# Adaptive average pooling on one core: GpSimd left out, each tile loaded as two column halves

## Chip, core and metric

The kernel runs on one core of one Trainium2 chip. The time is device microseconds of one execution; the figure for a kernel is the median of several runs. The core has TensorE (not used here), VectorE (DVE), ScalarE (ACT), GpSimd (POOL), SyncE (SP, which here issues all DMAs) and 16 DMA engines that move data between HBM and the on-chip memory SBUF of 128 partitions.

## What is computed

The input x has 32 x 256 rows of 4,096 float32 (134 MB). Each row is cut into 256 windows of 16 numbers, and the output holds the mean of each window (8.4 MB).

```python
batch, channels, length = 32, 256, 4096      # x: float32
output_size = 256
for i in range(output_size):
    start = int(i * length / output_size)
    end = int((i + 1) * length / output_size)
    result[:, :, i] = np.mean(x[:, :, start:end], axis=-1)
```

## The kernel before

The 8,192 rows are worked in 16 tiles of 512 rows, four rows to a partition. A tile is 128 partitions x 16,384 numbers: 64 KB in each partition, contiguous in HBM, 8.39 MB in all. The first 15 tiles are laid out so that a partition has 60 consecutive rows of x, of which tile t takes rows 4t to 4t+3; their results gather in one buffer `res_many` (61,440 B per partition) and leave in one store. The last tile has its own result buffer `res_last`.

The pool `inpool` (L53) has two input buffers. Each has 64 numbers more than a tile, and the last tile is put 32 numbers into its buffer (L65).

The loop over tiles (L62) does, for each tile:
- L73: SP issues one load of the whole tile. It waits until the buffer's last reader, the reduce at L84 two tiles earlier, is done.
- L74, L58: in the last tile, right after its load, SP issues the store of `res_many`, which waits for the scaling of tile 14.
- L76: GpSimd adds, for the second half of the tile's 1,024 windows, the upper 8 numbers of each window onto the lower 8, in place.
- L81: VectorE sums the first 512 windows, 16 numbers each.
- L84: VectorE sums the second 512 windows, of which GpSimd has left 8 numbers each. It waits for L76.
- L87: ScalarE multiplies the 1,024 sums by 1/16, after L84.

After the loop (L92, L93) the last tile's results are stored as partitions 0 to 119 and 120 to 127. SP then waits for the three stores (L98). The dependences between engines come from the tile framework; each engine works through its own instructions in program order.

Of the kernel before, what the change touches and what calls it, by code (L numbers as in the profile page):

```python
# [1 line left out]

# [4 lines left out]


@with_exitstack
def kernel(  # L10
    ctx: ExitStack,
    tc: tile.TileContext,
    x: bass.AP,
    output_size: int,
    out: bass.AP,
):

    nc = tc.nc
    F32 = mybir.dt.float32
    X = mybir.AxisListType.X

    batch, channels, length = x.shape
    ob, oc, olen = out.shape
    assert ob == batch and oc == channels and olen == output_size
    assert length % output_size == 0
    window = length // output_size  # L30
    hw = window // 2
    inv_w = 1.0 / float(window)

    P = nc.NUM_PARTITIONS
    R = 4
    rows = batch * channels
    assert rows % (P * R) == 0
    ntiles = rows // (P * R)
    many = (ntiles - 1) * R
    cells = R * output_size  # L40
    m = cells // 2
    cols = R * length

    xr = x.rearrange("b c l -> (b c) l")
    orow = out.rearrange("b c o -> (b c) o")
    x_many = xr[0 : P * many, :].rearrange("(p r) l -> p (r l)", p=P, r=many)
    o_many = orow[0 : P * many, :].rearrange("(p r) o -> p (r o)", p=P, r=many)
    x_last = xr[P * many :, :].rearrange("(p r) l -> p (r l)", p=P, r=R)
    o_last = orow[P * many :, :].rearrange("(p r) o -> p (r o)", p=P, r=R)

    res_many = nc.alloc_sbuf_tensor("res_many", [P, (ntiles - 1) * cells], F32, align_bytes=256)
    res_last = nc.alloc_sbuf_tensor("res_last", [P, cells], F32, align_bytes=256)
    inpool = ctx.enter_context(tc.tile_pool(name="inpool", bufs=2))  # L53

    stored = nc.alloc_semaphore("stored")

    def store(out, in_):
        ins = nc.sync.dma_start(out=out, in_=in_)  # L58
        tc.no_tile_sem_insts.add(ins.ins.name)
        ins.then_inc(stored, 16)  # L60

    for t in range(ntiles):  # L62
        last = t == ntiles - 1
        xbuf = inpool.tile([P, cols + 64], F32, name="xin")
        off = 32 if last else 0  # L65
        flat = xbuf[:, off : off + cols]
        xin = flat.rearrange("p (o w) -> p o w", w=window)
        if last:
            res, base, src = res_last, 0, x_last
        else:  # L70
            res, base = res_many, t * cells
            src = x_many[:, t * cols : (t + 1) * cols]
        nc.sync.dma_start(out=flat, in_=src)  # L73
        if last:  # L74
            store(o_many, res_many[:, :])
        nc.gpsimd.tensor_add(  # L76
            out=xin[:, m:cells, 0:hw],
            in0=xin[:, m:cells, 0:hw],
            in1=xin[:, m:cells, hw:window],
        )  # L80
        nc.vector.reduce_sum(  # L81
            out=res[:, base : base + m], in_=xin[:, 0:m, :], axis=X
        )
        nc.vector.reduce_sum(  # L84
            out=res[:, base + m : base + cells], in_=xin[:, m:cells, 0:hw], axis=X
        )
        nc.scalar.mul(  # L87
            out=res[:, base : base + cells],
            in_=res[:, base : base + cells],
            mul=inv_w,  # L90
        )
    for lo, hi in ((0, 120), (120, P)):  # L92
        store(o_last[lo:hi, :], res_last[lo:hi, :])  # L93

    ctx.pop_all().close()
    tc.close()
    tc.compile()  # L97
    nc.sync.wait_ge(stored, 48)  # L98
    nc.sync.sem_clear(stored)


# [1 line left out]
_INS = ['x', 'output_size']  # L103
_OUTS = [((32, 256, 256), 'float32')]

_NUMBERS = {'output_size': 256}


# [26 lines left out]
```

## Time and profile before

| what | value |
|---|---|
| time, median of 3 runs | 333.39 us (333.32 to 333.48) |
| span of the profiled execution | 332.2 us |
| VectorE busy | 209.7 us in 32 instructions |
| GpSimd busy | 139.7 us |
| ScalarE busy | 18.2 us |
| L76 GpSimd add, one | 8.719 us, 16 of them |
| L81 VectorE sum of 16, one | 8.686 us, 16 of them |
| L84 VectorE sum of 8, one | 4.420 us, 16 of them |
| L87 ScalarE scaling, one | 1.056 us, 16 of them |
| HBM read, written | 134.22 MB, 8.39 MB |

The profile is of one execution; its times are microseconds from the start of its span. "Busy" leaves out waiting and the issuing of DMAs. In a group's line the bracket at the end tells how long the engine was idle before the instruction and what ended that wait. A DMA packet is one contiguous row moved by one DMA engine. The DMA share is the time of the packets that start in a stretch, over the time of 16 engines in it, so in a short stretch it can be far above 1.

### The profile page before, as it was taken

Reading aid. Unit: us, or ns where it says so; the run is one execution under the profiler, and the core shown is the slowest. Engines: PE = TensorE matmul, PEld = TensorE weight load, DVE = VectorE, ACT = ScalarE, POOL = GpSimd, SP = SyncE. Lnnn points to the kernel's source line nnn. Section 1 sums busy time; section 2 is a strip of 40 time slices with the busy share of each in tenths; the row PEclk is TensorE's granted clock in tenths of the full one; section 3 lists DMA queues with packets and bytes.
Section 4 is the critical chain, followed back from the end, with each engine's and each line's share of the span. In section 5 each row is a group of like instructions: output and inputs, shape, how many; then the busy total and the mean of one; then the engine's idle time right before and its main releaser. Section 6 shows DMA issues by size and latency. Waiting matters only on the chain.

```text
span 332.2 us, 160 instructions
## 1 busy us (share of the span) xinstructions
DVE 209.7 (63%) x32; ACT 18.2 (5%) x17; POOL 139.7 (42%) x20
## 2 busy tenths in 40 slices
DVE  0029396692939669392956939295683929578392
ACT  1000101000010100001010000101000010101001
POOL 0027090642709064370906337090633709063370
DMA  9898989989898999989898998989899998989897
GB/s 379 379 505 379 505 379 442 442 379 505 379 505 379 481 402 402 481 379 505 379 497 387 466 418 379 505 379 505 379 489 395 418 466 379 505 379 505 363 473 300
DMA packets 2599, 142.61 MB, mean 429 GB/s; under 512 B 295, under 2 KB 295, under 8 KB 423
## 3 DMA queue, kind: packets, MB, share of 16 engines
q1 hardware_dynamic: 2599, 142.61, 99.4%
HBM read 134.22 MB, written 8.39 MB: 429 GB/s over the span
## 4 chain that ended last, share of the span: by engine, by line
DMA 66%; POOL 18%; DVE 11%; POOLq 3%; issue 0%; ACT 0%; SPq 0%
DMA xin<-in_x_dram 66%; POOL xin L76 18%; DVE res_many L84 9%; POOLq L97 3%; DVE res_last L84 1%; ACT res_last L87 0%; SPq L73 0%; POOLq L76 0%
## 5 line engine op out<-in xcount | busy, mean ns | idle before, releaser
L76 POOL TENSOR_TENSOR xin<-xin 128x4096 f32<-128x4096 f32 x16 | 139.5, 8719 | 181.9 <-DMA xin<-in_x_dram 181.9
L81 DVE TENSOR_REDUCE res_many<-xin 128x512 f32<-128x8192 f32 x15 | 130.3, 8686 | 107.3 <-DMA xin<-in_x_dram 107.3
L84 DVE TENSOR_REDUCE res_many<-xin 128x512 f32<-128x4096 f32 x15 | 66.3, 4420 | 2.5 <-POOL xin L76 2.3
L87 ACT ACTIVATE res_many<-res_many 128x1024 f32<-128x1024 f32 x15 | 15.8, 1056 | 289.6 <-DVE res_many L84 289.6
L81 DVE TENSOR_REDUCE res_last<-xin 128x512 f32<-128x8192 f32 x1 | 8.7, 8686 | 6.6 <-DMA xin<-in_x_dram 6.6
L84 DVE TENSOR_REDUCE res_last<-xin 128x512 f32<-128x4096 f32 x1 | 4.4, 4420 | 0.2 <-POOL xin L76 0.2
L87 ACT ACTIVATE res_last<-res_last 128x1024 f32<-128x1024 f32 x1 | 1.1, 1056 | 18.8 <-DVE res_last L84 18.8
L87 ACT ACT_TABLE_LOAD x1 | 1.3, 1283 | 0.7 <-PEq L116 0.7
L116 POOL MEMSET const-float32-0.0<- 128x1 f32 x1 | 0.1, 99 | 0.2 <-issue 0.2
L116 POOL MEMSET const-bfloat16-1.0<- 128x1 bf16 x1 | 0.1, 102 | 0.0
L116 POOL MEMSET const-uint8-127<- 128x1 uint8 x1 | 0.1, 102 | 0.0
L116 POOL MEMSET const-float32-1.0<- 128x1 f32 x1 | 0.1, 99 | 0.0
## 6 DMA issues: line engine op xcount, KB each, us to landing
out_dram<-res_many SPq DMA_DIRECT2D x1, 7680.0 KB
out_dram<-res_last SPq DMA_DIRECT2D x1, 480.0 KB
xin<-in_x_dram SPq DMA_DIRECT2D x16, 25.3
out_dram<-res_last SPq DMA_DIRECT2D x1, 32.0 KB
```

The source lines that it names most:

```text
L76: nc.gpsimd.tensor_add(out=xin[:, m:cells, 0:hw], in0=xin[:, m:cells, 0:hw], in1=xin[:, m:cells, hw:window],)
L81: nc.vector.reduce_sum(out=res[:, base : base + m], in_=xin[:, 0:m, :], axis=X)
L84: nc.vector.reduce_sum(out=res[:, base + m : base + cells], in_=xin[:, m:cells, 0:hw], axis=X)
L87: nc.scalar.mul(out=res[:, base : base + cells], in_=res[:, base : base + cells], mul=inv_w,)
L97: tc.compile()
L116: nc = _bacc.Bacc("TRN2", target_bir_lowering=False, num_devices=1)
```

## The change

GpSimd's add is removed. Each tile is loaded by two DMAs, one for each half of its columns (32 KB per partition, 4.19 MB), each into a buffer of its own; the pool has four buffers of that size, without the padding and without the shift of the last tile. VectorE sums each half with one instruction over windows of 16. Scaling and stores are as before; the store of `res_many` follows the second load of the last tile.

```diff
-    inpool = ctx.enter_context(tc.tile_pool(name="inpool", bufs=2))
+    inpool = ctx.enter_context(tc.tile_pool(name="inpool", bufs=4))
...
+    half = cols // 2
+    hm = cells // 2
     for t in range(ntiles):
         last = t == ntiles - 1
-        xbuf = inpool.tile([P, cols + 64], F32, name="xin")
-        off = 32 if last else 0
-        flat = xbuf[:, off : off + cols]
-        xin = flat.rearrange("p (o w) -> p o w", w=window)
         if last:
             res, base, src = res_last, 0, x_last
         else:
             res, base = res_many, t * cells
             src = x_many[:, t * cols : (t + 1) * cols]
-        nc.sync.dma_start(out=flat, in_=src)
+        parts = []
+        for k in range(2):
+            xbuf = inpool.tile([P, half], F32, name="xin")
+            nc.sync.dma_start(out=xbuf, in_=src[:, k * half : (k + 1) * half])
+            parts.append(xbuf)
         if last:
             store(o_many, res_many[:, :])
-        nc.gpsimd.tensor_add(
-            out=xin[:, m:cells, 0:hw],
-            in0=xin[:, m:cells, 0:hw],
-            in1=xin[:, m:cells, hw:window],
-        )
-        nc.vector.reduce_sum(
-            out=res[:, base : base + m], in_=xin[:, 0:m, :], axis=X
-        )
-        nc.vector.reduce_sum(
-            out=res[:, base + m : base + cells], in_=xin[:, m:cells, 0:hw], axis=X
-        )
+        for k, xbuf in enumerate(parts):
+            xin = xbuf.rearrange("p (o w) -> p o w", w=window)
+            at = base + k * hm
+            nc.vector.reduce_sum(out=res[:, at : at + hm], in_=xin, axis=X)
         nc.scalar.mul(
             out=res[:, base : base + cells],
             in_=res[:, base : base + cells],
             mul=inv_w,
         )
```

More of the change, by code (lines that the diff above doesn't have):

```diff
@@ L30 @@
     window = length // output_size
-    hw = window // 2
     inv_w = 1.0 / float(window)
@@ L40 @@
     cells = R * output_size
-    m = cells // 2
     cols = R * length
```

## The prediction

> **What bounds the kernel now.** I read the page first, for the load of each engine and the chain of waits that ended last.
>
> ```profile
> DVE 209.7 (63%) x32; ACT 18.2 (5%) x17; POOL 139.7 (42%) x20
> DMA packets 2599, 142.61 MB, mean 429 GB/s; under 512 B 295, under 2 KB 295, under 8 KB 423
> q1 hardware_dynamic: 2599, 142.61, 99.4%
> DMA 66%; POOL 18%; DVE 11%; POOLq 3%; issue 0%; ACT 0%; SPq 0%
> ```
>
> The third line says that the packets of the one DMA queue fill 99.4% of the time of 16 DMA engines. The fourth, the chain, gives GpSimd and VectorE 29% of the span. These two cannot both be limits, so I went to the timeline of one tile in the middle.
>
> ```profile
> 41.83 8.69 DVE L81 TENSOR_REDUCE res_many<-xin 128x512 f32<-128x8192 f32 x1 [6.08 <-DMA xin<-in_x_dram]
> 41.88 8.72 POOL L76 TENSOR_TENSOR xin<-xin 128x4096 f32<-128x4096 f32 x1 [10.58 <-DMA xin<-in_x_dram]
> 50.63 4.42 DVE L84 TENSOR_REDUCE res_many<-xin 128x512 f32<-128x4096 f32 x1
> 55.08 0.33 SPq L73 DMA_DIRECT2D xin<-in_x_dram  x1
> 55.08 1.06 ACT L87 ACTIVATE res_many<-res_many 128x1024 f32<-128x1024 f32 x1 [18.24 <-DVE res_many L84]
> 61.17 8.69 DVE L81 TENSOR_REDUCE res_many<-xin 128x512 f32<-128x8192 f32 x1 [6.13 <-DMA xin<-in_x_dram]
> ```
>
> Tile 1 lands at 41.8 and its buffer is free at 55.06, when the load of tile 3 is issued. Tile 2 was queued long before and lands only at 61.17, so the new load is queued 61.17 - 55.08 = 6.1 us before the DMA engines run dry. The chain passes through GpSimd and VectorE because the load of tile 3 waited for them, but the DMA engines did not wait for that load. Third, the end.
>
> ```profile
> 293.08 8.69 DVE L81 TENSOR_REDUCE res_many<-xin 128x512 f32<-128x8192 f32 x1 [6.02 <-DMA xin<-in_x_dram]
> ...
> 307.48 0.35 SPq L58 DMA_DIRECT2D out_dram<-res_many  x1
> 312.96 8.69 DVE L81 TENSOR_REDUCE res_last<-xin 128x512 f32<-128x8192 f32 x1 [6.59 <-DMA xin<-in_x_dram]
> ...
> 327.35 0.74 SPq L58 DMA_DIRECT2D out_dram<-res_last  x2
> ```
>
> The big store of 7.86 MB is issued at 307.48, before the last tile lands at 312.96. What is left to know is whether it keeps the DMA engines busy beyond 327.35, and what a packet costs. The view of busy time by stretch counts a packet in the stretch where it starts, so a stretch of 0.01 us catches single packets.
>
> ```profile
> 1.70:1.80 0.10, 0.00 (x0) 0.10 (x1) 0.00 (x0) 1.00 9.91 3277
> ...
> 306.70:306.71 0.01, 0.00 (x0) 0.01 (x1) 0.00 (x0) 1.00 15.11 6554
> 312.01:312.02 0.01, 0.00 (x0) 0.00 (x0) 0.00 (x0) 1.00 0.06 0
> 312.02:312.03 0.01, 0.00 (x0) 0.00 (x0) 0.00 (x0) 1.00 14.17 6144
> 327.86:327.87 0.01, 0.00 (x0) 0.00 (x0) 0.00 (x0) 1.00 14.17 6144
> 330.40:330.41 0.01, 0.00 (x0) 0.00 (x0) 0.00 (x0) 1.00 0.99 410
> 330.75:331.25 0.50, 0.00 (x0) 0.00 (x0) 0.00 (x0) 1.00 0.95 393
> ```
>
> The last two numbers are the DMA share and GB/s. 6554 GB/s in 0.01 us is one packet of 64 KB (a row of a tile), and its share 15.11 x 0.01 us x 16 engines is 2.418 us. 6144 is one row of the big store, 61,440 B, 14.17 x 0.16 = 2.267 us. 410 is one row of the last store, 4,096 B, 0.99 x 0.16 = 0.158 us. A share of 0.06 at 0 GB/s is one of the 295 tiny packets that tell of a completion, 0.06 x 0.16 = 0.0096 us. Rows of the big store still start at 327.86, 4 KB rows run until past 331.25. From the first packets at 1.7 us to about 331.8 the DMA engines have no hole: they bound the kernel, and all else lies beside them.
>
> **The change part by part.** The time is the bytes plus what packets and loads cost, so I price those first.
>
> *Twice as many packets.* 16 tiles x 128 rows of 64 KB are 2,048 packets; halves make 4,096 of 32 KB, that is 128 more on each of 16 engines. No packet of 32 KB is in the trace, so its fixed cost is bounded from rows of other sizes. Start to start: store rows start at 312.02 and 327.86, seven steps, 2.263 us each. The 4 KB rows run at 393 GB/s on 15 engines (120 rows, 8 each), which is 15 x 4096 / 393 = 0.156 us. The difference, 2.107 us for 57,344 B, is 36.74 ns per 1,000 B; 4,096 B take 150.5 ns of it and 5.5 ns are left as the fixed cost of a packet. Check: a 64 KB row should take 2.413 us, and tiles land every (293.08 - 41.83) / 13 = 19.327 us, 2.416 for each of 8 rows with the change of load included. From the durations (2.267 and 0.158) the fixed part is 7 to 9 ns with the rounding, but packets overlap: 8 x 2.418 + 0.0096 = 19.354 us does not fit into 19.327. So the upper bound is 128 x 9 ns = +1.15 us, the lower is nothing (it is lapped by the neighbour), and I take the start-to-start row because starts are what the rate is made of: 128 x 5.5 ns = +0.70 us.
>
> The Trainium skill, page "DMA: Bandwidth & Descriptors", section "Why small descriptors are slow (HBM only)", gives about 3 bus cycles per packet; with the 850 MHz of its table of specifications that is an estimate of 3.5 ns, or 128 x 3.5 = 0.45 us, and the time would be 334.0 instead of 334.2. The rows here show 5.5 ns, so the trace agrees in kind and I stay with the rows.
>
> *Sixteen more loads.* Each adds a completion packet of 0.0096 us per engine: 16 x 0.0096 = +0.15 us, at least nothing. On SP each adds an issue of 0.33 us and a wait for a reduce, some 5 us more in a queue that idles nearly all the time.
>
> *When loads are issued.* A half lands every 9.7 us and its reduce ends 8.75 us later; then SP may refill the buffer. Behind the wait on SP stand only later loads and the big store. Three other halves are then in the queue, 3 x 9.7 - 8.75 = 20.3 us of cover against 6.1 before. Priced at nothing; without the cover each load would restart the queue, which at the start takes from the issue at 0.73 to the first packets at 1.7, about 1.0 us.
>
> *VectorE does all sums.* Two instructions of the form of L81 (8.686 us) replace L81 and L84 (13.1 us): 32 x 8.686 = 278 us in a span of 332. Per half 8.7 of 9.7 us, so about 0.95 us idle remains; hidden behind the transfers. L81 runs beside GpSimd today and L84 alone, and both take about 1.06 ns per element of a row (8.686/8192, 4.420/4096 with its start), so I expect nothing from GpSimd's absence.
>
> *GpSimd out, the end.* After the last landing 327.35 - 312.96 = 14.4 us pass to the last stores; now one reduce and the scaling, 8.69 + 1.06 + 0.1 = 9.85. The last stores are issued 4.5 us sooner after landing, but queue behind the big store, whose rows start until about 327.9 and run to 330.1. Worth nothing. The big store itself is issued about 9.5 us before the last landing (one tile of 19.4 less 8.75 and 1.06) instead of 5.5; it only waits longer in the queue. The 128-byte shift of the last tile and the padding go: rows of the last tile took 2.418 us (306.70) with them, and the row at 282.55 of the tile before it without the shift has the same share, so nothing.
>
> *Sum.* Span 332.2 + 0.70 + 0.15 = 333.05. The median of the runs, 333.39, is 1.19 over the profiled span, which gives 334.24, said as 334.2; with the bounds 333.39 to 334.7.
>
> **The rivals.**
> - *Not slower: the fixed cost is lapped.* Place: between two packets of one engine. Durations exceed the step between starts by some 3 ns, so part is lapped already; if short packets lap all of it, the price is 0 and the time 333.4. It decides if a 32 KB row starts less than 1.208 us after the last. Against it: the 4 KB rows show 5.5 ns unlapped.
> - *Faster: the end is set by the work after the last landing.* The chain says so (GpSimd and VectorE after 312.96). Then 4.5 us go and 0.85 come: 329.7. It needs the store queue empty before the last stores are issued; the row at 327.86 and the 4 KB rows after 330 say that it is not.
> - *Each added load restarts the queue.* 16 x 1.0 us, 349.4. The 15 changes of load in the trace cost some 10 ns each, since the next load is queued. It decides only if fewer than one half were left in the queue. [...]
> - *VectorE becomes the bound.* It needs reduces over 9.7 us, 11% longer than any in the trace. At 10 us: the first half landed at 12.8 (the first tile lands at 22.5 today, less 9.7), 32 x 10.0, the scaling's 1.06, and 332.2 - 327.35 = 4.85 from the last stores to the end, 338.7 of span, 339.9. No row speaks for it.
>
> **How the numbers follow.** About 0.2% (0.67 us) is what a measurement of this kernel tells from no change. Forecast 0.62, with its own range 333.9 to 334.7; four fifths of it lie above 334.06. Lapped 0.20; end shortened 0.07; restart 0.04; VectorE or a cost that I do not see 0.07. Slower: 0.50 + 0.11 = 0.61; same: 0.12 + 0.20 = 0.32; faster 0.07. The range 333.3 to 335.0 takes in both bounds of the packet cost and a little of an unseen cost; the far rivals (0.15) lie mostly outside.
>
> **What would show it.** About 4,900 packets (4,096 + 256 + 551 tiny). In single-packet stretches a share near 7.6 for 32 KB (1.21 us). Tiles landing every 19.38 us instead of 19.327. VectorE near 280 us with about 0.95 us idle before each reduce, all ended by a landing. The last stores issued near 323.7, with rows of the big store still starting after that. The forecast is wrong if the step of a tile is not 0.05 us longer, if VectorE's idle time before reduces vanishes, or if the DMA engines show a hole between halves.

## The result and the profile after

| | median | runs |
|---|---|---|
| before | 333.47 us | 12 (333.32 to 333.80) |
| changed | 334.25 us | 12 (333.83 to 334.46) |

The ratio of changed to before is 1.0022, 95% interval 1.0013 to 1.003: slower by 0.78 us. The profiled execution has a span of 332.5 us, against 332.2 before. Measured again in two other sets of runs, the changed kernel took 333.85 us (1.0010, interval 1.0002 to 1.0019) and 333.73 us (1.0004, interval 0.9990 to 1.0019). The change costs between 0.3 and 0.8 us; every set has it above the kernel before, the last within its interval. The span is steadier than the time: in all three sets the changed kernel's spans have a median of 332.4 or 332.5 us, 0.3 above those of the kernel before. What differs from set to set is the part of the time that lies outside the span.

From the page of the changed kernel: VectorE's busy time, packets, queue, chain of waits, and the group of its sums.

```profile
DVE 278.0 (84%) x32; ACT 18.2 (5%) x17; POOL 0.2 (0%) x4
DMA packets 4903, 142.61 MB, mean 429 GB/s; under 512 B 551, under 2 KB 551, under 8 KB 679
q1 hardware_dynamic: 4903, 142.61, 99.5%
DMA 75%; DVE 21%; SPq 0%; ACT 0%; issue 0%
L79 DVE TENSOR_REDUCE res_many<-xin 128x512 f32<-128x8192 f32 x30 | 260.6, 8686 | 41.7 <-DMA xin<-in_x_dram 41.7
```

VectorE does a third more work, GpSimd none, and the DMA queue is as full as before, with the same bytes in nearly twice the packets. All that VectorE ever waits for is a landing. Two stretches of the timeline, in the middle and at the end:

```profile
41.86 8.69 DVE L79 TENSOR_REDUCE res_many<-xin 128x512 f32<-128x8192 f32 x1 [0.99 <-DMA xin<-in_x_dram]
...
51.54 8.69 DVE L79 TENSOR_REDUCE res_many<-xin 128x512 f32<-128x8192 f32 x1 [0.99 <-DMA xin<-in_x_dram]
...
293.56 8.69 DVE L79 TENSOR_REDUCE res_many<-xin 128x512 f32<-128x8192 f32 x1 [0.99 <-DMA xin<-in_x_dram]
...
303.36 0.34 SPq L56 DMA_DIRECT2D out_dram<-res_many  x1
312.93 8.69 DVE L79 TENSOR_REDUCE res_last<-xin 128x512 f32<-128x8192 f32 x1 [0.99 <-DMA xin<-in_x_dram]
...
322.73 0.91 SPq L56 DMA_DIRECT2D out_dram<-res_last  x2
```

Every reduce but the first waits about 0.99 us for its half. From 41.86 to 293.56 there are 26 halves, 9.681 us each, 19.362 us a tile. The last stores are issued 9.80 us after the last reduce starts, instead of 14.4. Yet the span does not shrink, and the single-packet stretches (DMA share and GB/s last) show why.

```profile
310.95:310.96 0.01, 0.01 (x1) 0.00 (x0) 0.00 (x0) 1.00 7.58 3277
312.17:312.18 0.01, 0.00 (x0) 0.00 (x0) 0.00 (x0) 1.00 14.17 6144
328.01:328.02 0.01, 0.00 (x0) 0.00 (x0) 0.00 (x0) 1.00 14.17 6144
```

A 32 KB row takes 7.58 x 0.16 = 1.213 us, two of them 2.426 against 2.418 for one of 64 KB. The big store's rows still start at 328.01, 2.267 us each, more than five microseconds after the last stores were issued: these wait in the queue.

### The profile page after: what moved, and what is told of

It reads as the page before. It is cut to its first block, busy times and chain, and to the rows that moved or that the text cites. A ratio compares the mean times of both kernels' runs of the same rounds, so it can differ in the third digit from the quotient of the medians.

```text
span 332.5 us, 158 instructions
## 1 busy us (share of the span) xinstructions
DVE 278.0 (84%) x32; ACT 18.2 (5%) x17; POOL 0.2 (0%) x4
## 2 busy tenths in 40 slices
DMA packets 4903, 142.61 MB, mean 429 GB/s; under 512 B 551, under 2 KB 551, under 8 KB 679
## 3 DMA queue, kind: packets, MB, share of 16 engines
q1 hardware_dynamic: 4903, 142.61, 99.5%
## 4 chain that ended last, share of the span: by engine, by line
DMA 75%; DVE 21%; SPq 0%; ACT 0%; issue 0%
DMA xin<-in_x_dram 75%; DVE res_many L79 18%; DVE res_last L79 3%; SPq L72 0%; ACT res_last L80 0%
## 5 line engine op out<-in xcount | busy, mean ns | idle before, releaser
L79 DVE TENSOR_REDUCE res_many<-xin 128x512 f32<-128x8192 f32 x30 | 260.6, 8686 | 41.7 <-DMA xin<-in_x_dram 41.7
L79 DVE TENSOR_REDUCE res_last<-xin 128x512 f32<-128x8192 f32 x2 | 17.4, 8686 | 2.0 <-DMA xin<-in_x_dram 2.0
```

Of the source, the lines that this page charges most:

```text
L79: nc.vector.reduce_sum(out=res[:, at : at + hm], in_=xin, axis=X)
```

## The experiments

Two theories. *Packets*: the DMA engines never pause, so the time is bytes plus a fixed cost for each packet and load. *Outside the span*: the profiled span grew by 0.3 us and the time by 0.78, so the rest (334.25 - 332.5 = 1.75 against 333.47 - 332.2 = 1.27) might come with GpSimd's absence or with the number of loads. Ratios below are to the kernel before in the same set of runs (333.42, 333.52 and 333.44 us).

### Two loads a tile, GpSimd kept

```diff
-        nc.sync.dma_start(out=flat, in_=src)
+        for k in range(2):
+            c = slice(k * cols // 2, (k + 1) * cols // 2)
+            nc.sync.dma_start(out=flat[:, c], in_=src[:, c])
```

> The kernel before with each tile loaded as two column halves into its one 64 KB buffer; GpSimd and VectorE work as before. Packets and loads alone: as in the changed kernel, 128 more packets per engine and 16 more loads, 334.1 to 334.3 us, one half landing every 9.68 us. If the part outside the span belongs to GpSimd's absence: span up by 0.3 and 333.7 to 333.8 us. If the packet cost is lapped: 333.5 us.

Measured: 334.04 us, ratio 1.0016 (1.0008 to 1.0025), span 332.4, halves landing every 9.68 us, 4,903 packets. With GpSimd and VectorE sharing the sums as before, the split of the loads alone costs 0.62 us (334.04 - 333.42), which lies within the 0.3 to 0.8 us of the whole change. The time is 0.06 us under the range that the packets were given, well above that of the other theory. But the 0.62 us are not all in the span: its median grew by 0.4 us (332.5 against 332.1), and the median time outside it is 1.56 us against 1.30, although GpSimd works here as before.

### GpSimd put back in one place

```diff
+            if t == 0 and k == 1:
+                hw = window // 2
+                nc.gpsimd.tensor_add(
+                    out=xin[:, :, 0:hw], in0=xin[:, :, 0:hw], in1=xin[:, :, hw:window]
+                )
+                xin = xin[:, :, 0:hw]
```

> The changed kernel with GpSimd's add put back in the second half of tile 0 alone (VectorE then sums 8 numbers there). Packet theory: no change, 334.2 us. If a program without GpSimd's work pays 0.47 us outside the span: 333.8 us at the same span of 332.5.

Measured: 334.05 us, 1.0017 (1.0008 to 1.0026), span 332.7. It lies between the two forecasts, and shows no gain from GpSimd's presence. Neither form of the second theory holds. The time outside the span has a median of 1.53 us here and 1.56 us in the halves with GpSimd at work, while the quarters and eighths below, with more loads and no GpSimd, have 1.33 and 1.31. The extra time outside the span is real all the same: in the later sets every execution of the kernel before has 1.25 to 1.35 us, and the changed kernel has a median of 1.75 us in its first set and of 1.35 and 1.34 in its two repeats. What makes it come and go stays open.

### Quarters and eighths

```diff
-    inpool = ctx.enter_context(tc.tile_pool(name="inpool", bufs=4))
+    inpool = ctx.enter_context(tc.tile_pool(name="inpool", bufs=8))
...
-    half = cols // 2
-    hm = cells // 2
+    half = cols // 4
+    hm = cells // 4
...
-        for k in range(2):
+        for k in range(4):
```

> The changed kernel with quarters: 16 KB rows, eight buffers, four reduces a tile. Per engine 256 packets and 32 loads more than the changed kernel. Packet theory: 256 x 4.7 ns + 32 x 0.007 = +1.4 us, 335.6 us (335.3 to 335.9), a tile every 19.45 us. If short packets lap their fixed cost: 334.2. If the time outside the span grows with the number of loads (0.47 for 16 of them): about 1 us more on top, 336.6.

Measured: 335.92 us, 1.0074 (1.0062 to 1.0087), span 334.7. The eighths are the same edit with 8 and 16 buffers.

> The changed kernel with eighths: 8 KB rows, 16 buffers, eight reduces a tile. Per engine 768 packets and 96 loads more than the changed kernel. Fixed cost per packet: 768 x 4.7 ns + 96 x 0.006 = +4.2 us, so 338.0 to 338.5 us. If the cost is not per packet but per load, as the quarters leave open (they gave +1.7 to +2.1 for 32 loads): 96 loads give +5 to +6, 339 to 340.

Measured: 338.86 us, 1.0157 (1.0143 to 1.0172), span 337.6. Packets and queues of the quarters, then of the eighths:

```profile
DMA packets 9513, 142.63 MB, mean 426 GB/s; under 512 B 1063, under 2 KB 1063, under 8 KB 1191
...
q1 hardware_dynamic: 9511, 142.61, 99.6%
q14 instruction: 2, 0.02, 0.0%
```

```profile
DMA packets 18730, 142.64 MB, mean 423 GB/s; under 512 B 2087, under 2 KB 2087, under 8 KB 2215
...
q1 hardware_dynamic: 18727, 142.61, 100.0%
q14 instruction: 3, 0.02, 0.0%
```

The load queue is full in all of them while the rate falls: short packets spend engine time on other things than bytes. Against the middle one of the three measurements of the changed kernel (333.85), quarters cost 2.07 us and eighths 5.01 us. The quarters lie just above their expectation; the eighths fall between their two.

Spread over the 256 and 768 packets that each engine has more, this would be 8.1 and 6.5 ns a packet, but two causes are mixed in that. The second is another queue, q14, named instruction, which the pages of the kernel before and of the changed kernel do not have. One of its two packets in the quarters starts here (it is 1.93 x 0.16 = 0.309 us long, and 819 GB/s in 0.01 us is 8 KB):

```profile
177.29:177.30 0.01, 0.01 (x1) 0.00 (x0) 0.00 (x0) 1.00 1.93 819
```

and these are VectorE's reduces around it:

```profile
173.41 4.42 DVE L79 TENSOR_REDUCE res_many<-xin 128x256 f32<-128x4096 f32 x1 [0.44 <-DMA xin<-in_x_dram]
178.99 4.42 DVE L79 TENSOR_REDUCE res_many<-xin 128x256 f32<-128x4096 f32 x1 [1.16 <-DMA xin<-in_x_dram]
183.83 4.42 DVE L79 TENSOR_REDUCE res_many<-xin 128x256 f32<-128x4096 f32 x1 [0.43 <-DMA xin<-in_x_dram]
```

Quarters land every 4.86 us, this one after 5.58. One row right behind that packet took 0.889 us instead of 0.611, and by the completion packets the last engine, 0.34 us behind the median one until then, is 0.90 us and more behind it from there to the end. A landing waits for the last engine, so a delay of one engine is paid in full. Around the other such packets (226.30 us in the quarters; 102.30, 117.39 and 259.89 us in the eighths) a row is held up in the same way. That these packets cause the delays is inferred from their place in time.

Apart from these places the landings are even: a tile lands every 19.45 us in the quarters and every 19.62 us in the eighths (by the completion packets 19.449 and 19.624), against 19.362 in the changed kernel. Over 16 tiles that is 1.4 and 4.2 us, just what 4.7 ns a packet and 6 to 7 ns a load had foreseen. The delays make up about 0.6 and 0.8 us more.

The starts of the packets also tell the cost of a packet from that of a load. Within a load an engine's rows start 2.414 us apart for 64 KB, 1.209 for 32 KB, 0.607 for 16 KB and 0.306 for 8 KB (the commonest steps in the traces). Two steps of one size less one step of the next larger are 4 to 5 ns each time, which is the cost of one more packet. From the last row of a load to the first of the next the step is 6 ns longer in all four. So the cost is not lapped, and it does not grow with shorter rows. The Trainium skill, page "DMA: Bandwidth & Descriptors", section "Why small descriptors are slow (HBM only)", names about 3 bus cycles per packet, at the page's 850 MHz an estimate of 3.5 ns; the traces agree in kind, with 4 to 5 ns.

### 64 KB rows without GpSimd

GpSimd's add is left out of the kernel before and L84 sums 16 numbers; the last tile alone comes as two halves.

```diff
-        nc.sync.dma_start(out=flat, in_=src)
+        if last:
+            for k in range(2):
+                c = slice(k * cols // 2, (k + 1) * cols // 2)
+                nc.sync.dma_start(out=flat[:, c], in_=src[:, c])
+        else:
+            nc.sync.dma_start(out=flat, in_=src)
...
-        nc.gpsimd.tensor_add(
-            out=xin[:, m:cells, 0:hw],
-            in0=xin[:, m:cells, 0:hw],
-            in1=xin[:, m:cells, hw:window],
-        )
...
-            out=res[:, base + m : base + cells], in_=xin[:, m:cells, 0:hw], axis=X
+            out=res[:, base + m : base + cells], in_=xin[:, m:cells, :], axis=X
```

> GpSimd left out, loads kept at 64 KB rows in two buffers; only the last tile comes as two column halves into its one buffer, so that the work after the last landing is one reduce of 8.7 us. If the time follows the packets alone: 8 more packets per engine x 5 ns = 0.04 us, so 333.5 us and a span of 332.2 to 332.3. If leaving GpSimd out costs the time that lies outside the span (334.25 - 332.5 = 1.75 in the changed kernel against 333.47 - 332.2 = 1.27): span as before and 333.9 to 334.0 us.

Measured: 351.66 us, 1.055 (1.0532 to 1.0568), span 349.6. Both theories failed, by 18 us. The timeline:

```profile
63.92 8.69 DVE L81 TENSOR_REDUCE res_many<-xin 128x512 f32<-128x8192 f32 x1 [4.62 <-DMA xin<-in_x_dram]
72.53 8.68 DVE L84 TENSOR_REDUCE res_many<-xin 128x512 f32<-128x8192 f32 x1
81.23 42.28 SPq L78 DMA_DIRECT2D xin<-in_x_dram  x3
...
83.30 8.69 DVE L81 TENSOR_REDUCE res_many<-xin 128x512 f32<-128x8192 f32 x1 [2.10 <-DMA xin<-in_x_dram]
...
105.88 8.69 DVE L81 TENSOR_REDUCE res_many<-xin 128x512 f32<-128x8192 f32 x1 [5.30 <-DMA xin<-in_x_dram]
```

and the DMA share around the issue at 81.23:

```profile
81.10:81.40 0.30, 0.10 (x1) 0.17 (x1) 0.00 (x0) 1.00 0.01 0
81.40:82.10 0.70, 0.00 (x0) 0.70 (x1) 0.00 (x0) 1.00 0.00 0
82.10:82.50 0.40, 0.00 (x0) 0.19 (x1) 0.00 (x0) 1.00 4.86 1638
```

The buffer comes free 17.3 us after its tile landed, and the next load is queued 2.07 us before the other tile is whole. That looked like enough for the 1.0 us from issue to first packet. But at 81.1 the first engines already write their completions (tiny packets at 0 GB/s) and have nothing left; the new packets start after 82.1. A landing is that of the slowest engine; the first ones ran dry about 2 us earlier. The next tile lands after 22.58 us instead of 19.33. From tile 0 to tile 14 the average is (309.50 - 22.72) / 14 = 20.48 us: five of the 14 steps are 2 to 3.5 us too long. The loads lose about 16 us in this way, and the rest lies at the end. So what GpSimd bought in the kernel before was the time at which a buffer comes free; with GpSimd kept and the last tile halved in the same way (below) nothing is lost.

### Fewer buffers of 32 KB

`bufs=4` becomes 3 or 2, nothing else.

> The changed kernel with three buffers: cover of 2 x 9.68 - 8.75 = 10.6 us. No restart: as the changed kernel, 333.8 to 334.3 us, one half every 9.681 us. If more loads in the queue are worth something by themselves: between 334 and 354.

Measured: 334.04 us, 1.0013 (0.9999 to 1.0028), every reduce as in the changed kernel: three are enough.

> The changed kernel with two buffers of 32 KB instead of four. A refill is queued 9.68 - 8.75 = 0.9 us before the queue is empty, against 1.0 us from an issue to its first packets, so the queue restarts at nearly every half. At 0.6 us for the slower first row, 31 x 0.6 = 20 us: 354 us (345 to 365). If only packets count and the queue forgives: 334.0.

Measured: 377.9 us, 1.1318 (1.1273 to 1.1362), far over the expected range. Its timeline, and its mean over a long stretch:

```profile
102.64 8.69 DVE L79 TENSOR_REDUCE res_many<-xin 128x512 f32<-128x8192 f32 x1 [4.31 <-DMA xin<-in_x_dram]
111.36 23.41 SPq L72 DMA_DIRECT2D xin<-in_x_dram  x3
112.83 8.69 DVE L79 TENSOR_REDUCE res_many<-xin 128x512 f32<-128x8192 f32 x1 [1.50 <-DMA xin<-in_x_dram]
...
125.72 8.69 DVE L79 TENSOR_REDUCE res_many<-xin 128x512 f32<-128x8192 f32 x1 [4.21 <-DMA xin<-in_x_dram]
```

```profile
60.00:300.00 240.00, 188.05 (x22) 11.46 (x11) 0.00 (x0) 1.00 0.93 375
```

VectorE waits 1.5 to 4.3 us before a reduce instead of 0.99, and the rate falls from 435 to 375 GB/s. A restart costs 44 / 31 = 1.4 us a half, not 0.6. I had priced the slower first row but not the engines that drift apart: the completion packets of one half lie 0.38 us apart in the changed kernel and up to 3.5 us here. A landing is that of the engine furthest behind, so the refill comes later for all.

### Why the span grew by less than the sum

In the kernel before, tiles 1 to 14 land every (293.08 - 22.53) / 14 = 19.325 us, but the last one took 19.88. The last row of each engine before the store, in the kernel before, by the share of the 16 packets that start in this stretch:

```profile
309.10:309.68 0.58, 0.00 (x0) 0.00 (x0) 0.00 (x0) 1.00 5.03 1808
```

This is 5.03 x 0.58 = 2.92 us a row, where others take 2.418; the changed kernel's last rows take 1.213 like all. Three runs look at that: the last tile alone as halves with GpSimd kept, the shift and padding left out, and the kernel before again.

```diff
-        nc.sync.dma_start(out=flat, in_=src)
+        if last:
+            for k in range(2):
+                c = slice(k * cols // 2, (k + 1) * cols // 2)
+                nc.sync.dma_start(out=flat[:, c], in_=src[:, c])
+        else:
+            nc.sync.dma_start(out=flat, in_=src)
```

> The kernel before, GpSimd kept, with only the last tile loaded as two column halves into its buffer. In the kernel before the last row of the last load takes 2.92 us instead of 2.42 on average; in the changed kernel no row there is stretched. If the size of the last rows before the store decides: the 0.49 us go, 8 packets x 5 ns and one load come, span 331.8 and 332.9 to 333.1 us, below the kernel before. If the stretch is made up by the store later: 333.4 us. It also is the control of the GpSimd-free run with 64 KB rows that took 351.66: with GpSimd there is no restart of the queue here.

Measured: 333.44 us, 0.9998 (0.9990 to 1.0007), span 332.0. The stretch did not go with the length of the rows: of the last 16 rows, now of 32 KB, eight took 1.27 to 1.57 us instead of 1.213.

```diff
-        xbuf = inpool.tile([P, cols + 64], F32, name="xin")
-        off = 32 if last else 0
+        xbuf = inpool.tile([P, cols], F32, name="xin")
+        off = 0
```

> The kernel before without the padding and the 32-number shift of the last tile. If the shift makes the stretch of the last rows: span 331.8, 333.0 us. Packet theory: nothing changes, 333.4 us, and the stretch stays.

Measured: 333.40 us, 0.9997 (0.9988 to 1.0006), span 332.1, the last tile 19.82 us after the one before: the shift neither makes the stretch nor costs anything.

> The kernel before, unchanged, for a second profile. Span 332.2 and 333.4 us; the last rows of the last load stretched again by some 0.5 us if that belongs to the kernel, not if it was chance in one execution.

Measured: 333.51 us, span 332.2. Three of its tiles:

```profile
61.49 8.69 DVE L81 TENSOR_REDUCE res_many<-xin 128x512 f32<-128x8192 f32 x1 [6.12 <-DMA xin<-in_x_dram]
...
81.02 8.69 DVE L81 TENSOR_REDUCE res_many<-xin 128x512 f32<-128x8192 f32 x1 [6.24 <-DMA xin<-in_x_dram]
...
100.35 8.69 DVE L81 TENSOR_REDUCE res_many<-xin 128x512 f32<-128x8192 f32 x1 [6.05 <-DMA xin<-in_x_dram]
```

Here the delay is elsewhere: 19.53 us between 61.49 and 81.02, 19.33 after it, and the last rows take 2.54 us. From the first landing to the last it is 312.96 - 22.53 = 290.43 us in one execution and 313.07 - 22.84 = 290.23 in the other, though the delays lie in different loads.

> The changed kernel, unchanged, for a second profile beside the others. 334.1 to 334.3 us, span 332.5, one half landing every 9.681 us. If the time outside the span is larger without GpSimd's work: above the 334.04 of the halves with GpSimd by 0.2 us or more.

Measured: 333.85 us, under the expected range; span 332.5, halves again every 9.681 us. And the third time:

> The changed kernel, unchanged, a third time: 333.8 to 334.3 us, 0.3 to 0.8 above the kernel before, span 332.5. It tells what the two earlier measurements (0.78 and 0.33 above) leave open.

Measured: 333.73 us, span 332.3, the same step. This lies just under the expected range.

So the kernel before loses about half a microsecond over a run to rows that now and then take longer: its undisturbed step is 19.319 us by the completion packets, and 15 of them are 289.8 us instead of 290.4 and 290.2. The kernels loaded in halves throughout lose almost none of that and pay the fixed cost of their packets instead. Why the long rows are held up stays open; neither the shift, nor one fixed place, nor the length of the last rows explains it. Halving the last tile alone changes the median span by 0.1 us (332.1 against 332.2) and no measured time. None of these kernels beats the kernel before.

## Why the prediction was right

It said 334.2 us, and 334.25 was measured, then 333.85 and 333.73. The direction and the mechanism held; that the first number agrees so closely is luck. The forecast was a span of 333.05 and 1.19 us outside it; the first set had 332.5 and 1.75. The span came out 0.55 us under its forecast and the rest 0.56 us over it.

- *The DMA engines bound the kernel and the chain's share of GpSimd is no gain.* Held: GpSimd's 8.7 us and L84 are off the chain and nothing was won.
- *Twice the packets, +0.70, and 16 loads, +0.15.* Both costs are there, somewhat smaller: 4 to 5 ns a packet instead of 5.5 and 6 ns a load instead of 9.6. An undisturbed tile takes 19.362 instead of 19.319 us, 16 x 0.043 = 0.69 us, where 0.85 was foreseen. The span grew by 0.3 us only, because the sum took the loads of the kernel before as undisturbed; they lose some 0.5 us that the halves do not lose.
- *The part outside the span, taken as the 1.19 us of the kernel before.* This was not held to be a term of the change, and in the first set it grew to 1.75 us, in the repeats to 1.35 and 1.34. No run shows why.
- *Cover of 20.3 us, priced at nothing.* Held: each reduce waits 0.99 us (0.95 foreseen), three buffers do as well, two do not.
- *VectorE 278 us.* Held: 278.0, at 8.686 us each with GpSimd silent.
- *The end worth nothing.* Held: the last stores 9.80 us after the last landing (9.85 foreseen), the big store issued 9.57 us ahead of it (9.5), and its rows still in the queue.
- *The rival of the restart.* Rightly given little chance here. Its condition, fewer than one half (9.7 us) left in the queue, is too wide: 6.1 us of rest were enough in the kernel before, while 2.07 us (64 KB rows without GpSimd) and 0.9 us (two buffers) were not. Where it happened it cost more than 1.0 us: 20.48 - 19.33 = 1.15 us a tile on average, and 1.4 us a half.
- *The rival that short packets lap their cost* fell: rows of 32 KB start 1.209 us apart, not under 1.208, and quarters and eighths cost 1.4 and 4.2 us by their steps.

## What to carry to other kernels

If the DMA share is 1.00 in the middle and a store still drains when the last results are ready, look at the packets, not at the engines: faster sums win nothing, and shorter rows cost a few nanoseconds each. Before dividing a difference of whole times by a number of packets, look whether the landings are even: one delayed engine is paid in full. An engine that is off the critical path can still hold a buffer: work out how long before the queue is empty its refill is issued, and count from the first DMA engine that runs dry, not from the landing. The Trainium skill, page "Perfetto Trace Analysis", section "DMA Optimizations", says that splitting transfers may let a task end sooner where the DMA engines are generally idle. Here they were not idle, and splitting alone did not help but cost 0.62 us, 0.4 of it in the span.

## What was not expected of the hardware

A load queued 2.07 us ahead of the landing still left a hole, since the first DMA engines finished about 2 us before the last; the restarts cost 1.15 us a tile on average (1.4 us a half with two buffers). Rows of 64 KB now and then took up to 3.2 us instead of 2.418; in the kernels loaded in halves throughout, nearly all rows of 32 KB took 1.213 to the end. A single 8 KB packet of the instruction queue was followed by a lasting delay of one engine, which every later landing then shows. It is still there in the last stores of the quarters, whose 4 KB rows are still starting here,

```profile
332.40:333.20 0.80, 0.00 (x0) 0.00 (x0) 0.00 (x0) 1.00 0.78 318
333.20:334.20 1.00, 0.00 (x0) 0.00 (x0) 0.00 (x0) 1.00 0.12 49
```

and the second stretch is almost empty: 0.12 of 16 engines is about two, the late ones, while the others have finished.
